# One-hot products on VectorE, and 28 blocks of early scores in plain float32 between the steps of a router

## The chip, the cores and the metric

The kernel runs on one core of a Trainium2 chip. The metric is the time of one execution in microseconds (us), taken on the device; a profile of one execution shows what each engine did. The engines are TensorE (PE; its weight loads are listed apart as PEld), VectorE (DVE), ScalarE (ACT), GpSimd (POOL) and SyncE (SP), which issues most transfers.

## The reference, cut to what matters

The program is a trunk of two layers over 512 tokens with 256 context tokens and 1024 channels. Each layer ends in a mixer with 16384 experts of one neuron each. A token has 8 heads; each head scores two halves of a query against two tables of 128 keys, takes the best 16 of each, combines the sums, and keeps the best 16 pairs as its experts:

```python
        qy = (xb @ w_q).reshape(t, PEER_HEADS, 2, PEER_DKEY // 2)
        s = jnp.einsum('thpd,hpnd->thpn', qy, sub_keys).astype(jnp.float32)
        s_top, i_top = lax.top_k(s, kk)
        comb = (s_top[:, :, 0, :, None] + s_top[:, :, 1, None, :]).reshape(t, PEER_HEADS, kk * kk)
        c_top, c_idx = lax.top_k(comb, kk)
        i1 = jnp.take_along_axis(i_top[:, :, 0], c_idx // kk, axis=-1)
        i2 = jnp.take_along_axis(i_top[:, :, 1], c_idx % kk, axis=-1)
        expert = i1 * PEER_KEYS + i2
        gate = jax.nn.softmax(c_top, axis=-1)
        u = u_tab[expert]
        vv = v_tab[expert]
        act = jax.nn.gelu(jnp.einsum('td,thkd->thk', xb, u).astype(jnp.float32), approximate=False)
        return jnp.einsum('thk,thkd->td', (gate * act).astype(xb.dtype), vv)
```

The kernel must return the latent stream after both layers.

## The kernel before, in words

Work goes by tiles of 128 tokens. For three of the four latent tiles (`ND = 3`, 384 tokens) the mixer isn't done by fetching rows, but densely: `peer_dense` walks over all 128 blocks of 128 experts. For each block it makes the scores of all 384 tokens (`expert_scores`), multiplies the GELU of them by a table of gates that is zero where a token hasn't chosen the expert (`gated`), and adds the products with `v` into six accumulators (`apply`). The fourth tile (and, in layer 0, both context tiles) is done by indirect transfers of single rows on POOL's queue; `pump` releases these gathers at `rate` per dense block, 3 in layer 0 and 2.5 in layer 1, and 2 in a block of `FILL`. Layer 1 ends its gathers with the last blocks; in layer 0 the rest of them runs beside the next mixer.

Float32 products are mostly made of three products in the type fp32r, a rounded form that the operand is split into: `uh` (rounded, on ACT, L1330) and `ul` (the rest, on POOL, L1331); the transposed input `xT` is held as two such parts. A block of scores so has 8 x 3 = 24 matmuls of 384 columns (`sp`), and a block of `apply` 3 x 2 x 3 = 18 of 512 columns (`acc`).

Ahead of the dense blocks stands `peer_route` (names begin with `xp` in layer 0, `yp` in layer 1): four groups of query matmuls and key scores with `top16` on DVE, then for every tile `chosen`, which runs `combine`, then `peer_gates`. `combine` picks indices by a one-hot comparison `oh` (L1180, DVE), a product (L1182, POOL) and a tree of additions (L1185, DVE). `peer_gates` makes the table of gates of a tile in 32 steps `q` of four tokens: a comparison `i2` (L1302, DVE), a comparison `o1` (L1305, DVE), a product `i1` of `o1` and the gates (L1308, POOL; the fourth token by ACT), and four plain float32 matmuls `pg` on PE, copied out by ACT.

The scores of the last 20 blocks (`FILL`) don't depend on the router. They are issued at low priority, in the same split form as in the dense stage, and fill PE's gaps in the router; their GELU goes to DRAM (`gedram`), and the dense stage reads it back, so that these blocks have only `apply` there. Engines take their instructions in program order; a scheduler that sorts by priority sets that order when the program is built.

Of the kernel before, what the change touches and what calls it, by code (L numbers as in the profile page):

```python
# [19 lines left out]
P = 128  # L20
# [7 lines left out]
FILL = range(P - 20, P)  # L28
# [12 lines left out]
class Trunk:  # L41
    def __init__(self, tc, ins, out, dbg=None):
        self.tc = tc
        self.nc = tc.nc
        self.I = ins
        self.out = out
        self.dbg = dbg or {}
        self.flip = 0
        self.queue = []
        self.aside = []  # L50
        self.rate = (3, 2.5)
        self.owed = 0
# [645 lines left out]
    def out_proj(self, yT, w, layer, s, xs, dst, nm, xT, nd):  # L698
# [3 lines left out]
        xh, xl = xT  # L702
        self.h2 = []
        with self.tc.tile_pool(name=nm + "_op", bufs=2, side="right") as tp:
# [35 lines left out]
            def turn(t, h):  # L740
                for g in range(2):
                    p = self.ps(nm + f"_o{t}h2T{g}")
                    for kb in range(4):
                        self.tr(p[:, kb * P:(kb + 1) * P], h[:, (4 * g + kb) * P:(4 * g + kb + 1) * P])
                    d = lambda q: q[:, 4 * g:4 * g + 4, t * P:(t + 1) * P]
                    pv = p.rearrange("p (k t) -> p k t", t=P)
                    nc.scalar.copy(d(xh), pv)
                    nc.vector.tensor_sub(d(xl), pv, d(xh))

# [265 lines left out]
    def peer_route(self, layer, nm, xT, nd, fill=None, beside=iter(())):  # L1015
# [6 lines left out]
        xh, xl = xT  # L1022
        with ExitStack() as st:
# [14 lines left out]
            with ExitStack() as qst:  # L1038
                w3 = qst.enter_context(self.tc.tile_pool(name=nm + "_prw", bufs=2))
                if fill:  # L1040
                    fill()
# [50 lines left out]
                aside(1 << 20)  # L1092
# [23 lines left out]
            with self.tc.tile_pool(name=nm + "_pg", bufs=2) as g2:  # L1116
                for t in order[:nt - nd + 1]:
                    weave(chosen(t))
                for t in range(nd):
                    weave(self.peer_gates(g2, picks, t, nm), *([chosen(t + 1)] if t + 1 < nd else []))  # L1120
        return res
# [10 lines left out]
    def combine(self, pool, p2, V, Iu, ex, gate, hs, nm):  # L1132
# [44 lines left out]
        for q, sel in ((0, isel), (1, jsel)):  # L1177

            oh = pool.tile(sh, BF16, tag=f"oh{q}", name=nm + f"_oh{q}")
            nc.vector.tensor_tensor(oh, sel.rearrange("p (h k) -> p h k", h=n).unsqueeze(2).to_broadcast(sh),  # L1180
                                    self.rank.unsqueeze(1).to_broadcast(sh), op=ALU.is_equal)
            nc.gpsimd.tensor_mul(oh, oh, I4[:, :, q, :].unsqueeze(3).to_broadcast(sh))  # L1182
            yield
            for w in (8, 4, 2):
                nc.vector.tensor_add(oh[:, :, 0:w, :], oh[:, :, 0:w, :], oh[:, :, w:2 * w, :])  # L1185
            nc.vector.tensor_add(ex[:, q, hs], oh[:, :, 0, :], oh[:, :, 1, :])
            yield
# [98 lines left out]
    def peer_gates(self, pool, picks, t, nm):  # L1286
# [8 lines left out]
        for g in range(4):  # L1295
            go = pool.tile([P, P, 32], F32, tag="go", name=nm + f"_go{t}{g}")
            for q in range(8):
# [10 lines left out]
                anchor = nc.gpsimd.tensor_mul(i1[:, 0:3, :], o1[:, :, 0:3].rearrange("p i e -> p e i"),  # L1308
# [8 lines left out]
                if q % 2:  # L1317
                    yield
            nc.sync.dma_start(self.gdram[4 * t + g], go)

    def expert_scores(self, pool, b, xT, layer, nm, ps):
# [3 lines left out]
        ur = pool.tile([P, D], F32, tag="ur", name=nm + f"_ur{b}")  # L1325
        nc.sync.dma_start(ur, self.I[f"peer_uT{layer}"][b])
# [93 lines left out]
    def peer_x(self, xs, dst, xT, layer, nm, done):  # L1420
        with ExitStack() as st:
            up = st.enter_context(self.tc.tile_pool(name=nm + "_du", bufs=2))

            def fill():

                with self.tc.high_priority(offset=-LATER // 2):
                    for i, b in enumerate(FILL):
                        go, _ = self.expert_scores(up, b, xT, layer, nm, self.acc)
                        self.nc.scalar.dma_start(self.gedram[i], go())

            with self.banks(nm + "r", 4, 2, 2):
                r = self.peer_route(layer, nm, xT, ND, fill=fill)
# [5 lines left out]
    def build(self):  # L1438
        nc, tc, I = self.nc, self.tc, self.I
        with ExitStack() as st:  # L1440
# [13 lines left out]
            with ExitStack() as l0:  # L1454
# [174 lines left out]
```

## Time and profile before

| | us |
|---|---|
| median of 3 runs | 4472.95 |
| lowest and highest of them | 4471.51, 4479.77 |
| the profiled execution | 4472.55 |
| its span in the trace | 4470.6 |
| PE, DVE, POOL, ACT busy in it | 3969.2, 3589.9, 2416.3, 1671.3 |

The profiled execution lies 0.4 us under the median, and 1.95 us of its time lie outside the span. In the tables of windows a line gives a stretch of the span, the busy time of each engine with its number of instructions, the clock granted to TensorE as a share of its full speed, the mean busy share of the 16 DMA engines, and what they moved. In a timeline a row gives start, duration, engine, line and operation, output and inputs, and in brackets the idle time before with what ended it; an instruction's recorded duration reaches past the start of the next one on its engine, so the spacing of starts says what it costs in a row of many.

### The profile page before, as it was taken

To read this page: it belongs to the slowest core of one execution; us is meant where nothing else is said; L and a number is where in the kernel's file an instruction comes from. 1 tells how busy PE (TensorE), PEld (TensorE's weight loads), DVE (VectorE), ACT (ScalarE), POOL (GpSimd) and SP (SyncE) were. 2 spreads that over 40 slices of the span, in tenths; PEclk is the share of its full clock that TensorE was granted. 3 is DMA by queue.
4 is the path that set the end of the run, shared out by engine and by line. 5 is a ranking of instruction groups with operands and counts; after the bars stand their busy time and mean duration, and the time that the engine had idled before them with its cause. 6 is when DMAs were issued, how large, how long until landed. Compare 5 with 4: busy or idle time off the path is not lost. (4 is left out here: it accounts for less than half of the span.)

```text
span 4470.6 us, 60041 instructions
## 1 busy us (share of the span) xinstructions
PE 3969.2 (89%) x20898; PEld 3312.4 (74%) x20898; DVE 3589.9 (80%) x6565; ACT 1671.3 (37%) x2981; POOL 2416.3 (54%) x1736
## 2 busy tenths in 40 slices
PE   7988988886786789999999976999767999999998
PEld 4676554784576678998999754776766899999997
DVE  1355889998899989999999876554999788888875
ACT  2354343452224533333333331652345333333333
POOL 0003567545646788767666765002467666666644
PEclk9999999998888999999999997999889999999999
DMA  8825589768822399999999987212224988888875
GB/s 305 293 89 167 195 299 326 265 218 270 290 92 109 164 363 350 346 341 337 336 345 337 319 288 255 65 59 88 71 114 170 354 318 304 306 313 308 308 259 174
DMA packets 480256, 1107.70 MB, mean 248 GB/s; under 512 B 38224, under 2 KB 251728, under 8 KB 470736
## 3 DMA queue, kind: packets, MB, share of 16 engines
q1 hardware_dynamic: 326592, 558.60, 36.0%
q0 software_dynamic: 147600, 537.40, 33.3%
q10 hardware_dynamic: 5760, 7.87, 0.5%
q8 instruction: 164, 2.69, 0.2%
q14 instruction: 140, 1.15, 0.1%
HBM read 1033.41 MB, written 70.78 MB: 247 GB/s over the span
## 5 line engine op out<-in xcount | busy, mean ns | idle before, releaser
L1331 POOL TENSOR_TENSOR yp_ul<-yp_ur,yp_uh 128x1024 fp32r<-128x1024 f32 x128 | 310.3, 2425 | 537.1 <-ACT yp_uh L1330 536.8
L74 PE MATMUL yp_sp<-yp_xT,yp_uh 128*128 128x384 f32 x2048 | 537.8, 343 | 9.8 <-ACT yp_ge L1340 8.3
L74 PE MATMUL xp_sp<-xp_xT,xp_uh 128*128 128x384 f32 x2048 | 536.3, 342 | 9.3 <-ACT xp_uh L1330 8.7
L1331 POOL TENSOR_TENSOR xp_ul<-xp_ur,xp_uh 128x1024 fp32r<-128x1024 f32 x128 | 316.9, 2477 | 162.5 <-ACT xp_uh L1330 161.6
L1221 POOL DMA_INDIRECT cp_v<-peer_v,cp_idx x256 | 311.8, 1218 | 166.4 <-DVE cp_acc L1250 100.1
L74 PEld LDWEIGHTS yp_sp<-yp_xT,yp_uh 128*128 128x128 f32 x2048 | 382.1, 193 | 20.0 <-ACT yp_ge L1340 9.7
L74 PEld LDWEIGHTS xp_sp<-xp_xT,xp_uh 128*128 128x128 f32 x2048 | 380.7, 192 | 18.9 <-ACT xp_uh L1330 9.3
L1221 POOL DMA_INDIRECT cp_u<-peer_u,cp_idx x256 | 319.2, 1247 | 134.2 <-issue 44.5
L74 PE MATMUL xp_sp<-xp_xT,xp_ul 128*128 128x384 f32 x1024 | 351.2, 343 | 21.3 <-POOL xp_ul L1331 21.3
L1378 DVE TENSOR_TENSOR yp_a<-yp_ge,yp_gb 128x384 f32<-128x384 f32 x108 | 257.8, 2387 | 139.9 <-ACT yp_ge L1340 139.9
L74 PE MATMUL yp_sp<-yp_xT,yp_ul 128*128 128x384 f32 x1024 | 352.2, 344 | 16.1 <-POOL yp_ul L1331 16.1
L1250 DVE SCALAR_TENSOR_TENSOR cp_acc<-cp_v,cp_act,cp_acc 128x1024 f32<-128x1024 f32 x254 | 330.5, 1301 | 7.1 <-DMA cp_v<-peer_v,cp_idx 4.4
L74 PE MATMUL xp_acc<-xp_vh,xp_al 128*128 128x512 f32 x768 | 309.3, 403 | 24.8 <-DVE xp_al L1383 23.7
L74 PE MATMUL xp_acc<-xp_vh,xp_ah 128*128 128x512 f32 x768 | 305.4, 398 | 17.3 <-ACT xp_ah L1382 17.3
L74 PE MATMUL xp_acc<-xp_vl,xp_ah 128*128 128x512 f32 x768 | 305.8, 398 | 3.5 <-POOL xp_vl L1370 3.5
L74 PE MATMUL yp_acc<-yp_vh,yp_al 128*128 128x512 f32 x768 | 301.1, 392 | 0.3 <-issue 0.3
L74 PE MATMUL yp_acc<-yp_vl,yp_ah 128*128 128x512 f32 x768 | 300.7, 392 | 0.0
L74 PE MATMUL yp_acc<-yp_vh,yp_ah 128*128 128x512 f32 x768 | 298.8, 389 | 0.3 <-ACT yp_ah L1382 0.3
L1378 DVE TENSOR_TENSOR xp_a<-xp_ge,xp_gb 128x384 f32<-128x384 f32 x108 | 236.2, 2187 | 49.0 <-ACT xp_ge L1340 49.0
L1330 ACT CAST yp_uh<-yp_ur 128x1024 fp32r<-128x1024 f32 x128 | 134.6, 1051 | 327.4 <-issue 235.0
L1330 ACT CAST xp_uh<-xp_ur 128x1024 fp32r<-128x1024 f32 x128 | 134.4, 1051 | 264.4 <-issue 167.4
L74 PEld LDWEIGHTS xp_sp<-xp_xT,xp_ul 128*128 128x128 f32 x1024 | 196.9, 192 | 23.4 <-POOL xp_ul L1331 23.4
(1460 smaller groups left out, 10491.4 us busy)
## 6 DMA issues: line engine op xcount, KB each, us to landing
xp_ur<-peer_uT SPq DMA_DIRECT2D x128, 512.0 KB
xp_vr<-peer_v SPq DMA_DIRECT2D x128, 512.0 KB
yp_ur<-peer_uT SPq DMA_DIRECT2D x128, 512.0 KB
yp_vr<-peer_v SPq DMA_DIRECT2D x128, 512.0 KB
aw<-ada_w SPq DMA_DIRECT2D x48, 1024.0 KB
gdram<-xp_go SPq DMA_DIRECT2D x12, 2048.0 KB
xp_gb<-gdram SPq DMA_DIRECT2D x32, 768.0 KB
gdram<-yp_go SPq DMA_DIRECT2D x12, 2048.0 KB
```

The costliest lines, as they stand in the source:

```text
L74: self.nc.tensor.matmul(out, lhsT, rhs, start=start, stop=stop)
L1221: d = nc.gpsimd.indirect_dma_start(out=r, out_offset=None, in_=tab, in_offset=bass.IndirectOffsetOnAxis(ap=idx[:, j:j + 1], axis=0))
L1250: i = nc.vector.scalar_tensor_tensor(acc, v, act[:, j:j + 1], acc, op0=ALU.mult, op1=ALU.add)
L1330: nc.scalar.copy(uh, uv)
L1331: anchor = nc.gpsimd.tensor_sub(ul, uv, uh)
L1378: nc.vector.tensor_mul(a.rearrange("p (g t) -> p g t", t=32), ge.rearrange("p (g t) -> p g t", t=32), gbs[b // 4][:, :, b % 4, :])
```

## The change

The change has four parts. `FILL` grows from 20 to 28 blocks. The scores of those blocks become 8 plain float32 matmuls per block, of `u` as loaded and of a third, float32 copy of the transposed input (`xT[2]`), without the split on ACT and POOL. They are no longer issued at low priority, but by a generator that `fills(k)` advances by hand: one step at the router's start, two after each step of a tile's choice and two after each pair of steps `q` in the gates, and the rest at the end. A step is one matmul; the block's last one comes with its GELU and its store. The loads of `u` run one block ahead. And the two products on one-hot tables, `oh` in `combine` (16 in each of the two latent routers, 8 in the context one) and `i1` in `peer_gates` (96 in each latent router), move from POOL to DVE.

```diff
-FILL = range(P - 20, P)
+FILL = range(P - 28, P)
...
                     nc.scalar.copy(d(xh), pv)
                     nc.vector.tensor_sub(d(xl), pv, d(xh))
+                    if t < nd:
+                        self.evac(d(xT[2]), pv)
...
-                if fill:
-                    fill()
+                self.fills(1)
...
-                aside(1 << 20)
+                while first:
+                    aside(1)
+                    self.fills(2)
...
                 for t in order[:nt - nd + 1]:
-                    weave(chosen(t))
+                    for _ in chosen(t):
+                        self.fills(2)
                 for t in range(nd):
                     weave(self.peer_gates(g2, picks, t, nm), *([chosen(t + 1)] if t + 1 < nd else []))
+                self.fills(1 << 20)
...
-            nc.gpsimd.tensor_mul(oh, oh, I4[:, :, q, :].unsqueeze(3).to_broadcast(sh))
+            nc.vector.tensor_mul(oh, oh, I4[:, :, q, :].unsqueeze(3).to_broadcast(sh))
...
-                anchor = nc.gpsimd.tensor_mul(i1[:, 0:3, :], o1[:, :, 0:3].rearrange("p i e -> p e i"),
+                anchor = nc.vector.tensor_mul(i1[:, 0:3, :], o1[:, :, 0:3].rearrange("p i e -> p e i"),
                                               pk[:, 2, t0:t0 + 3].unsqueeze(2).to_broadcast([P, 3, P]))
...
                 if q % 2:
+                    self.fills(2)
                     yield
...
+    def load_u(self, pool, b, layer, nm):
+        ur = pool.tile([P, D], F32, tag="ur", name=nm + f"_ur{b}")
+        self.nc.sync.dma_start(ur, self.I[f"peer_uT{layer}"][b])
+        return ur
+
+    def fills(self, k):
+
+        while k and next(self.fill, 0) != 0:
+            k -= 1
...
-                with self.tc.high_priority(offset=-LATER // 2):
-                    for i, b in enumerate(FILL):
-                        go, _ = self.expert_scores(up, b, xT, layer, nm, self.acc)
-                        self.nc.scalar.dma_start(self.gedram[i], go())
-
+                load = lambda b: self.load_u(up, b, layer, nm)
+                nxt = load(FILL[0])
+                yield
+                for i, b in enumerate(FILL):
+                    ur, nxt = nxt, load(b + 1) if i + 1 < len(FILL) else None
+                    sp = self.acc(nm + f"_sp{b}")
+                    for k in range(KD):
+                        self.mm(sp[:, :ND * P], ur[:, k * P:(k + 1) * P], xT[2][:, k, :], start=(k == 0), stop=(k == KD - 1))
+                        if k < KD - 1:
+                            yield
+                    ge = up.tile([P, ND * P], F32, tag="ge", name=nm + f"_ge{b}")
+                    self.nc.scalar.activation(ge, sp[:, :ND * P], AF.Gelu)
+                    self.nc.scalar.dma_start(self.gedram[i], ge)
+                    yield
+
+            self.fill = fill()
```

Where the matmuls stand decides what PE can do while it waits. The first place is PE's program in layer 1 where the first tile's choice is turned round (`pk`) and the gates begin. Here 24 split products a block stand before it, 264 of them since the last key scores:

```order
L74 MATMUL yp_sp_25210<-yp_xT_24532,yp_uh_25206 128x384
L74 MATMUL yp_sp_25210<-yp_xT_24531,yp_ul_25207 128x384
L74 MATMUL yp_sp_25210<-yp_xT_24531,yp_uh_25206 128x384
L77 MATMUL yp_pk_26926<-ident,yp_ex_24813 128x128
L74 MATMUL yp_sp_25210<-yp_xT_24532,yp_uh_25206 128x384
L74 MATMUL yp_sp_25210<-yp_xT_24531,yp_ul_25207 128x384
L74 MATMUL yp_sp_25210<-yp_xT_24531,yp_uh_25206 128x384
L74 MATMUL yp_sp_25210<-yp_xT_24532,yp_uh_25206 128x384
L77 MATMUL yp_pk_26926<-ident,yp_ex_24813 128x128
L77 MATMUL yp_pk_26926<-ident,yp_gate_24817 128x128
L74 MATMUL yp_sp_25210<-yp_xT_24531,yp_ul_25207 128x384
L74 MATMUL yp_sp_25210<-yp_xT_24531,yp_uh_25206 128x384
```

After the change the same place holds plain products with `yp_ur` and `yp_xTf`, and 91 of them stand since the last key scores:

```order
L75 MATMUL yp_sp_26096<-yp_xTf,yp_ur_25932 128x384 x8
L75 MATMUL yp_sp_26233<-yp_xTf,yp_ur_26094 128x384 x8
L78 MATMUL yp_pk_25851<-ident,yp_ex_24297 128x128
L75 MATMUL yp_sp_26353<-yp_xTf,yp_ur_26231 128x384
L78 MATMUL yp_pk_25851<-ident,yp_ex_24297 128x128
L78 MATMUL yp_pk_25851<-ident,yp_gate_24301 128x128
L75 MATMUL yp_sp_26353<-yp_xTf,yp_ur_26231 128x384 x5
L75 MATMUL yp_0_pg<-yp_0_i_25868,yp_0_i_25864 128x128 x4
L75 MATMUL yp_sp_26353<-yp_xTf,yp_ur_26231 128x384
L75 MATMUL yp_4_pg<-yp_4_i_25881,yp_4_i_25877 128x128 x4
L75 MATMUL yp_sp_26353<-yp_xTf,yp_ur_26231 128x384
```

From there on, a fill product stands between most gate products. The second place is PE in the third tile's gates of layer 1, before the change:

```order
L74 MATMUL yp_88_pg<-yp_88_i_28223,yp_88_i_28219 128x128 x4
L74 MATMUL yp_92_pg<-yp_92_i_28236,yp_92_i_28232 128x128 x4
L74 MATMUL yp_96_pg<-yp_96_i_28251,yp_96_i_28247 128x128 x4
L74 MATMUL yp_100_pg<-yp_100_i_28264,yp_100_i_28260 128x128 x4
L74 MATMUL yp_sp_25380<-yp_xT_24532,yp_uh_25376 128x384
L74 MATMUL yp_104_pg<-yp_104_i_28277,yp_104_i_28273 128x128 x4
L74 MATMUL yp_108_pg<-yp_108_i_28290,yp_108_i_28286 128x128 x4
L74 MATMUL yp_112_pg<-yp_112_i_28303,yp_112_i_28299 128x128 x4
L74 MATMUL yp_116_pg<-yp_116_i_28316,yp_116_i_28312 128x128 x4
L74 MATMUL yp_120_pg<-yp_120_i_28329,yp_120_i_28325 128x128 x4
```

and with it:

```order
L75 MATMUL yp_88_pg<-yp_88_i_27302,yp_88_i_27298 128x128 x4
L75 MATMUL yp_sp_27496<-yp_xTf,yp_ur_27480 128x384
L75 MATMUL yp_92_pg<-yp_92_i_27315,yp_92_i_27311 128x128 x4
L75 MATMUL yp_96_pg<-yp_96_i_27332,yp_96_i_27328 128x128 x4
L75 MATMUL yp_sp_27496<-yp_xTf,yp_ur_27480 128x384
L75 MATMUL yp_100_pg<-yp_100_i_27345,yp_100_i_27341 128x128 x4
L75 MATMUL yp_sp_27496<-yp_xTf,yp_ur_27480 128x384
L75 MATMUL yp_104_pg<-yp_104_i_27363,yp_104_i_27359 128x128 x4
L75 MATMUL yp_sp_27496<-yp_xTf,yp_ur_27480 128x384
L75 MATMUL yp_108_pg<-yp_108_i_27376,yp_108_i_27372 128x128 x4
L75 MATMUL yp_112_pg<-yp_112_i_27394,yp_112_i_27390 128x128 x4
```

Before, the gate products stand nearly bare there; now a plain fill product lies between most of them, some 109 over all 96 steps, and 22 to 24 are left before the first `acc`, where 100 split ones were left before. The third place is DVE at the same steps, before:

```order
L1302 TENSOR_TENSOR yp_92_i_28232<-yp_picks_27739,iota 128x512
L1305 TENSOR_TENSOR yp_92_o_28234<-yp_iotam,yp_pb_27926 128x512
L1302 TENSOR_TENSOR yp_96_i_28247<-yp_picks_27739,iota 128x512
L1305 TENSOR_TENSOR yp_96_o_28249<-yp_iotam,yp_pb_27926 128x512
L1302 TENSOR_TENSOR yp_100_i_28260<-yp_picks_27739,iota 128x512
L1305 TENSOR_TENSOR yp_100_o_28262<-yp_iotam,yp_pb_27926 128x512
```

and after, where L1308, L1311 and L1314 are the lines of `i2`, `o1` and the product `i1`:

```order
L1311 TENSOR_TENSOR yp_96_o_27330<-yp_iotam,yp_pb_26965 128x512
L1308 TENSOR_TENSOR yp_100_i_27341<-yp_picks_26755,iota 128x512
L1314 TENSOR_TENSOR yp_96_i_27332<-yp_96_o_27330,yp_picks_26755 128x384
L1311 TENSOR_TENSOR yp_100_o_27343<-yp_iotam,yp_pb_26965 128x512
L1308 TENSOR_TENSOR yp_104_i_27359<-yp_picks_26755,iota 128x512
L1314 TENSOR_TENSOR yp_100_i_27345<-yp_100_o_27343,yp_picks_26755 128x384
L1311 TENSOR_TENSOR yp_104_o_27361<-yp_iotam,yp_pb_26965 128x512
L1308 TENSOR_TENSOR yp_108_i_27372<-yp_picks_26755,iota 128x512
L1314 TENSOR_TENSOR yp_104_i_27363<-yp_104_o_27361,yp_picks_26755 128x384
```

The product has become a third DVE instruction of each step, one step behind its comparison.

## Rows read from the trace of the kernel before

**Rows 1.** Windows of layer 1: choice, gates, transition, normal dense blocks, FILL blocks.

```profile
3185.00:3275.00 90.00, 59.64 (x278) 57.15 (x277) 89.28 (x380) 29.59 (x37) 43.86 (x22) 0.79 0.26 89
3275.00:3457.00 182.00, 137.36 (x887) 118.18 (x886) 178.81 (x290) 99.75 (x207) 129.42 (x105) 0.93 0.36 148
3457.00:3485.00 28.00, 24.73 (x127) 24.09 (x125) 6.78 (x6) 10.69 (x15) 18.80 (x11) 0.88 0.95 357
3485.00:4366.00 881.00, 880.66 (x4451) 801.50 (x4452) 735.60 (x704) 307.66 (x424) 544.47 (x357) 1.00 0.85 305
4366.00:4456.00 90.00, 90.00 (x399) 74.27 (x397) 49.63 (x54) 33.63 (x46) 46.86 (x19) 1.00 0.60 197
```

**Rows 2.** Windows of layer 0: choice and gates, normal dense blocks, FILL blocks.

```profile
1299.00:1571.00 272.00, 195.15 (x1162) 174.55 (x1161) 270.20 (x676) 131.41 (x242) 174.33 (x126) 0.89 0.32 126
1610.00:2525.00 915.00, 895.23 (x4455) 806.12 (x4456) 844.87 (x837) 312.80 (x433) 667.59 (x444) 0.99 0.94 343
2525.00:2648.00 123.00, 99.23 (x395) 75.47 (x393) 111.57 (x87) 30.25 (x41) 101.62 (x59) 0.96 0.90 307
```

**Rows 3.** Timeline of DVE in the choice of layer 1, the two comparisons of one tile.

```profile
3210.11 0.68 DVE L1180 TENSOR_TENSOR yp_c_oh<-yp_c10isel,rank 128x1024 bf16<-128x1024 bf16 x1
3211.07 2.25 DVE L1180 TENSOR_TENSOR yp_c_oh<-yp_c10jsel,rank 128x1024 bf16<-128x1024 bf16 x1
```

**Rows 4.** Timeline of DVE in the gates of layer 0.

```profile
1506.04 0.68 DVE L1302 TENSOR_TENSOR xp_i<-xp_picks,iota 128x512 f32<-128x512 f32 x1
1506.65 1.04 DVE L1305 TENSOR_TENSOR xp_o<-xp_iotam,xp_pb 128x512 bf16<-128x512 bf16 x1
1507.62 0.68 DVE L1302 TENSOR_TENSOR xp_i<-xp_picks,iota 128x512 f32<-128x512 f32 x1
```

**Rows 5.** Lines L1305 and L1308 in layer 1 (min/median/max in ns).

```profile
L1305 DVE TENSOR_TENSOR yp_o<-yp_iotam,yp_pb x96: 401/1045/2582, 3273.3 to 3453.0; 128x512 bf16<-128x512 bf16 x96
...
L1308 POOL TENSOR_TENSOR yp_i<-yp_o,yp_picks x96: 826/1146/1391, 3273.8 to 3454.1; 128x384 f32<-128x384 bf16 x96
```

**Rows 6.** Timeline of PE in the same gates of layer 0.

```profile
1504.32 1.16 PE L74 MATMUL xp_pg<-xp_i,xp_i 128*128 128x128 f32 x8 [0.41 <-POOL xp_i L1308]
```

**Rows 7.** Timeline of PE in a normal dense block, first and last products.

```profile
4303.86 0.51 PE L74 MATMUL yp_sp<-yp_xT,yp_uh 128*128 128x384 f32 x2
...
4308.05 0.39 PE L74 MATMUL yp_acc<-yp_vh,yp_ah 128*128 128x512 f32 x1
...
4311.94 0.39 PE L74 MATMUL yp_acc<-yp_vh,yp_al 128*128 128x512 f32 x1
```

**Rows 8.** Groups of DVE in the choice, layer 1 (count, busy us, mean ns).

```profile
L1185 DVE TENSOR_TENSOR yp_c_oh<-yp_c_oh 128x512 bf16<-128x512 bf16 x9 | 12.1, 1346 | 0.0
L1185 DVE TENSOR_TENSOR yp_c_oh<-yp_c_oh 128x256 bf16<-128x256 bf16 x10 | 9.0, 904 | 0.0
```

**Rows 9.** Timeline of DVE: the same forms at their shortest, later.

```profile
3375.11 0.41 DVE L1185 TENSOR_TENSOR yp_c_oh<-yp_c_oh 128x512 bf16<-128x512 bf16 x1
3376.68 0.28 DVE L1185 TENSOR_TENSOR yp_c_oh<-yp_c_oh 128x256 bf16<-128x256 bf16 x1
```

**Rows 10.** Timeline of DVE, products of 384 and 1024 elements elsewhere.

```profile
2734.67 0.55 DVE L823 TENSOR_TENSOR m_qr_t<-m_qr_rot,sin 128x384 f32<-128x384 f32 x1
2735.14 0.55 DVE L824 TENSOR_TENSOR m_qrt<-m_qrt,cos 128x384 f32<-128x384 f32 x1
...
2764.10 1.22 DVE L1253 TENSOR_TENSOR xp_acc<-xp_acc,xp_g 128x1024 f32<-128x1024 f32 x1
```

**Rows 11.** Timeline and window of PE: 12 plain float32 products; timeline: first turn in layer 1.

```profile
2738.71 7.90 PE L74 MATMUL m_qn<-cqT,m_wuq 128*128 128x384 f32 x24
...
2738.50:2747.00 8.50, 8.12 (x26) 4.45 (x24) 8.43 (x13) 0.83 (x2) 4.87 (x4) 1.00 0.97 319
...
3269.71 0.45 PE L77 MATMUL yp_pk<-ident,yp_ex 128*128 128x128 f32 x1 [8.84 <-DVE yp_ex L1186]
```

**Rows 12.** Gathers of layer 0 left behind the dense stage (line L1221, count, first, last).

```profile
L1221 POOL DMA_INDIRECT xp_v<-peer_v,xp_idx x44: 944/1244/1962, 2669.4 to 2754.0; - x44
```

More of the change, by code (lines that the diff above doesn't have):

```diff
@@ L49, in __init__ @@
         self.queue = []
+        self.fill = iter(())
         self.aside = []
@@ L701, in out_proj @@
         nc = self.nc
-        xh, xl = xT
+        xh, xl = xT[:2]
         self.h2 = []
@@ L1012, in odd_mixer, with peer_route @@
         return xT
-    def peer_route(self, layer, nm, xT, nd, fill=None, beside=iter(())):
+    def peer_route(self, layer, nm, xT, nd, beside=iter(())):
         nc = self.nc
@@ L1021, in peer_route @@
         res = []
-        xh, xl = xT
+        xh, xl = xT[:2]
         with ExitStack() as st:
@@ L1324, in expert_scores @@
         n = ND * P
-        ur = pool.tile([P, D], F32, tag="ur", name=nm + f"_ur{b}")
-        nc.sync.dma_start(ur, self.I[f"peer_uT{layer}"][b])
+        ur = self.load_u(pool, b, layer, nm)
         uh = pool.tile([P, KD, P], F32R, tag="uh", name=nm + f"_uh{b}")
@@ L1424, in fill @@
             def fill():
-                with self.tc.high_priority(offset=-LATER // 2):
-                    for i, b in enumerate(FILL):
-                        go, _ = self.expert_scores(up, b, xT, layer, nm, self.acc)
-                        self.nc.scalar.dma_start(self.gedram[i], go())
+                load = lambda b: self.load_u(up, b, layer, nm)
[13 more added lines that the diff above has]
+            self.fill = fill()
             with self.banks(nm + "r", 4, 2, 2):
-                r = self.peer_route(layer, nm, xT, ND, fill=fill)
+                r = self.peer_route(layer, nm, xT, ND)
             with self.banks(nm + "d", 2, 6):
@@ L1474, in f @@
                         p = st.enter_context(tc.tile_pool(name=name, bufs=1))
-                        return [p.tile([P, KD, n], F32R, name=name + str(j)) for j in range(2)]
+                        return [p.tile([P, KD, n], F32R, name=name + str(j)) for j in range(2)] + \
+                            ([p.tile([P, KD, ND * P], F32, name=name + "f")] if n == NX else [])
                     return f
```

## The prediction

> **What bounds the kernel now.** I cut the span of layer 1 into windows at the places where a stage's first instruction stands, then read timelines inside them. In the normal dense blocks PE is busy for 880.66 of 881 us and in the `FILL` blocks for 90.00 of 90, at full clock [rows 1]: these are bound by PE, and what leaves PE leaves the time. Between the last key scores and the first `acc` it is otherwise. In the choice (90 us) DVE is busy for 89.28 and PE for 59.64; in the gates (182 us) DVE for 178.81 and PE for 137.36; in the transition (28 us) PE has most, 24.73 [rows 1]. So the router's 300 us hang on DVE for 272 and on PE for 28. Layer 0 has the same for choice and gates, 272 us with DVE at 270.20 [rows 2]. Its dense stage differs: with three gathers a block DVE and the DMA engines are nearly full too (915 us for 108 blocks, 8.5 a block), and in `FILL` DVE has 111.57 and POOL 101.62 of 123 us, PE only 99.23: the gathers pace it.
>
> DVE's busy time in the router is not all work. The comparison `oh` of one tile takes 0.68 us, and its twin, while POOL runs the product on the first, 2.25 [rows 3]. In the gates `o1` takes 0.40 us at its shortest and 1.05 in the median, with POOL's `i1` at 1.15 [rows 5]. In the steady part a step costs 0.61 for `i2` and 0.97 for `o1`, 1.58 together [rows 4], and PE waits 0.41 us of it for POOL's `i1` [rows 6]. DVE and POOL hold each other up there.
>
> **Price of a score block.** The 24 split products take 4308.05 - 4303.86 = 4.19 us, and the 18 of `acc` (4311.94 - 4308.05) / 17 x 18 = 4.12 [rows 7], so a normal block is 8.3 and a `FILL` block 4.1. The trace has plain float32 products of 384 columns: 24 records, two for each product, in 7.90 us at granted clock 1.00 [rows 11]. Less the last one's tail (some 0.17) that is 0.322 a record, 0.644 a product, 5.15 us a block of 8. By itself a plain block is 0.96 dearer than a split one, where PE is the bound.
>
> The row has two records for a product that costs 3.7 times one of the split products (0.175). [...] I take the row's 5.15.
>
> **Router, choice (L1 90 us).** Off DVE go the mutual waits: three `oh` comparisons at 2.3 instead of 0.68 make 4.9 us [rows 3]; the additions L1185 of 512 and 256 elements average 1.346 and 0.904 us here against 0.41 and 0.28 at their shortest, so 9 x 0.94 + 10 x 0.62 = 14.7 [rows 8, 9]. Other forms have some of it too; I count none. On DVE come 8 products `oh`. Two bounds: 0.60 us, the comparison of the same size, and 1.22, a 1024-element product in float32 [rows 3, 10]. An operand that is repeated over 16 elements makes the second nearer: 8 x 1.2 = 9.6. DVE then has 89.3 - 19.6 + 9.6 = 79; with the mutual waits that I didn't count I take 73 as the middle between that and 67. PE has 91 plain products, 58.6 us, and an idle end like the 8.84 us ahead of the first turn [rows 11]: 67. So 73, a gain of 17; bounds 67 and 79.
>
> **Gates (L1 182 us).** The nearest row for `i1` on DVE is a float32 product of 384 elements: 0.55 recorded, 0.47 from start to start [rows 10]; from above, POOL's own shortest, 0.83 [rows 5]. The size, the output type and the engine agree with the first, so 0.47. A step on DVE is then 0.61 + 0.33 (`o1`, 0.40 recorded) + 0.47 = 1.40, and 96 of them 134. What else stands on DVE there is 178.8 - 96 x 1.58 = 27, and 4 products `oh` add 5, less some waiting: in all 162 to 166. PE has 96 steps of four gate products, recorded as 1.16 with a tail of some 0.2 [rows 6], so about 1.0 each and 96 in all, and 109 fill products at 0.644, 70: 166. The two engines are level, at 165, a gain of 17. POOL, with neither `ul` nor `i1`, has nearly nothing left there. ACT loses 20 casts `uh` and keeps the copies; it was busy for 99.75 of 182.
>
> **Transition (28 us).** Of 148 split products ahead of the first `acc` some 100 belonged to `FILL`: 17.5 us; now 22 plain ones, 14.2, plus nothing else new: 3 less. The loads of 28 blocks, 512 KB each, fall into stages with a DMA share of 0.26 and 0.36 [rows 1], which cover them.
>
> Layer 1's router: -17 - 17 - 3 = -37. Layer 0's has the same counts within three products and the same windows: -36, for a transition that waits more on its loads.
>
> **Dense, layer 1.** Eight blocks lose 24 split products: 8 x 4.19 = -33.5. Gathers: 8 blocks now get 2 instead of 2.5, and about 6 of 256 land in `FILL` blocks. Layer 0's `FILL` blocks show what two gathers do to a block without scores: 123 us for 22 groups of `acc`, 5.6 instead of 4.1 [rows 2, 1], 0.75 a gather: +4.5. Together -29.
>
> **Dense and tail, layer 0.** Eight blocks go from 8.5 to 5.6: -23. But each releases one gather less, so 8 more of the 512 slots stay behind the dense stage. There 44 of them stand at (2754.0 - 2669.4) / 43 = 1.97 us [rows 12], and the next mixer waits for the last: +16. Together -7. The gain of this stage is mostly handed to the tail.
>
> **Small parts.** The six extra evacuations of `xT[2]` a layer stand at the end of a projection: +1 in all. The context router's 8 products move beside the latent mixer, which keeps PE busy: 0.
>
> **Sum**: -37 - 36 - 29 - 7 + 1 = -108. The profiled execution is 4472.55, 0.4 under the median, so 4472.55 - 108 = 4365.
>
> **Rivals.**
> (B) More of DVE's time was waiting, and PE isn't in the way: choice 63, gates 155 (DVE's 134 and 21), so -27 - 27 - 4 = -58 a router and 4365 - 43 = 4322. For it: L1185 is not the only form that is long beside POOL. Against: PE's own count of 166 in the gates.
> (C) `i1` on DVE costs what it cost on POOL, since it reads `o1` across its rows: 0.83. A step is 0.61 + 0.33 + 0.83 = 1.77, the gates 170 + 30 = 200, 18 longer than now; a router is then -17 + 18 - 3 = -2 and the time 4472.55 - 4 - 35 = 4434. The gates lose from (182 - 30) / 96 - 0.94 = 0.64 us on. For it: no row has this stride on DVE.
> (D) PE is dearer than the row: its granted clock, 0.79 in the choice and 0.93 in the gates [rows 1], stays as low. Then 58.6 / 0.79 + 8.8 = 83 and 166 / 0.93 = 178, 10 + 13 more a router: 4365 + 46 = 4411. Against: the clock is low there where PE waits, and the fill products now stand between the waits. [...]
> (E) Slower. PE takes its instructions in order, and now a fill product stands between most gate products. A block whose `ur` hasn't landed holds up the gate products behind it, and with them the copies on ACT and the four buffers of `i1` that DVE writes. Each of 56 blocks has a load of 512 KB with only one block's lead. It decides from 108 / 56 = 1.9 us of open wait a block; at 4 us it gives 4365 + 224 = 4589. Against: a block's 8 products are spread over some 8 steps of 1.4 to 1.7 us, so a load has over 11 us, and the DMA engines are two thirds idle.
>
> **Chances.** Forecast 0.62, B 0.10, C 0.11, D 0.12, E 0.05. The range 4325 to 4412 takes in D and the bounds of the choice (6 each way and router) and leaves out C, E and half of B, 0.2. A measurement of this kernel tells about 0.2%, 9 us. All but E, and the edge of C with a dearer `oh` too, lie below that: faster 0.94, same 0.02, slower 0.04.
>
> **What the profile after would show.** Right: windows of choice and gates of about 73 and 165 us a layer, with PE over 0.9 busy in the gates; `o1` near 0.4 and `i1` on DVE near 0.55 recorded; plain fill products 0.64 apart; layer 1's dense part 29 shorter; the end of layer 0's gathers no more than 10 earlier after the router's gain is taken off. Wrong: `i1` at 0.8 or more (C), PE idle ahead of `yp_sp` with a DMA of `yp_ur` as releaser (E), fill products 0.7 or more apart at full clock, or a granted clock of 0.8 in the gates (D).

## The result, and the profile after

The changed kernel takes 4371.97 us (median of 4 runs, 4360.89 to 4380.56) against 4476.01 before: ratio 0.9771, 95% interval 0.9757 to 0.9784. Forecast were 4365 and a range of 4325 to 4412. The profiled execution took 4360.89, 11 under the median and 111.7 less than the profiled one of before, while the medians differ by 104; differences of a few us between stages of two profiles mean little, above all in layer 0's dense stage.

Windows of layer 1 after the change, with the columns of [rows 1]: choice, gates, transition, normal dense blocks, `FILL` blocks.

```profile
3133.10:3206.20 73.10, 65.50 (x200) 37.99 (x199) 72.35 (x388) 19.96 (x29) 2.23 (x1) 0.95 0.37 119
3206.20:3361.60 155.40, 155.06 (x974) 124.02 (x973) 154.16 (x390) 96.94 (x208) 0.00 (x0) 1.00 0.56 210
3361.60:3392.00 30.40, 25.28 (x95) 18.13 (x95) 7.31 (x4) 9.07 (x13) 10.24 (x7) 0.94 0.89 311
3392.00:4210.20 818.20, 815.40 (x4118) 740.66 (x4117) 692.16 (x672) 284.57 (x392) 523.74 (x346) 1.00 0.87 312
4210.20:4344.80 134.60, 126.60 (x541) 101.85 (x541) 87.23 (x80) 44.97 (x62) 75.03 (x33) 0.99 0.66 222
```

The same five of layer 0, for [rows 2]:

```profile
1286.40:1358.90 72.50, 65.78 (x202) 38.53 (x201) 72.32 (x383) 19.56 (x29) 2.23 (x1) 0.95 0.36 111
1358.90:1515.20 156.30, 155.75 (x978) 124.89 (x977) 156.27 (x396) 97.81 (x209) 1.54 (x1) 1.00 0.55 209
1515.20:1563.80 48.60, 29.15 (x100) 20.80 (x99) 28.11 (x40) 9.25 (x12) 25.62 (x20) 0.75 1.00 367
1563.80:2403.30 839.50, 820.96 (x4117) 740.82 (x4117) 780.23 (x775) 283.89 (x393) 626.50 (x410) 1.00 0.94 344
2403.30:2570.20 166.90, 137.67 (x542) 107.42 (x540) 157.01 (x118) 43.08 (x57) 138.76 (x83) 0.93 0.93 320
```

In the choice DVE is the engine without a gap, as before, but it needs 73 us instead of 90 [rows 1]; PE is busy for 65.50 of them. In the gates PE (155.06) and DVE (154.16) are both full for 155.40 us and POOL does nothing at all. Groups by line in layer 1, for [rows 5], show the price of a comparison, of `i1` and of `oh` on DVE (min/median/max in ns):

```profile
L1311 DVE TENSOR_TENSOR yp_o<-yp_iotam,yp_pb x96: 394/418/423, 3203.9 to 3359.4; 128x512 bf16<-128x512 bf16 x96
L1314 DVE TENSOR_TENSOR yp_i<-yp_o,yp_picks x96: 528/551/558, 3204.8 to 3359.8; 128x384 f32<-128x384 bf16 x96
L1188 DVE TENSOR_TENSOR yp_c_oh<-yp_c_oh,yp_c_If x13: 1209/1212/1220, 3146.4 to 3287.3; 128x1024 bf16<-128x1024 bf16 x13
```

The comparison's longest is now 423 ns where its median was 1045. Timelines of DVE and of PE in the gates, for [rows 4, 6]: a step is 1.40 us from `o1` to `o1`, a pair of plain records 0.64.

```profile
3300.19 0.42 DVE L1311 TENSOR_TENSOR yp_o<-yp_iotam,yp_pb 128x512 bf16<-128x512 bf16 x1
3300.52 0.69 DVE L1308 TENSOR_TENSOR yp_i<-yp_picks,iota 128x512 f32<-128x512 f32 x1
3301.12 0.55 DVE L1314 TENSOR_TENSOR yp_i<-yp_o,yp_picks 128x384 f32<-128x384 bf16 x1
3301.59 0.42 DVE L1311 TENSOR_TENSOR yp_o<-yp_iotam,yp_pb 128x512 bf16<-128x512 bf16 x1
```

```profile
3305.87 0.81 PE L75 MATMUL yp_sp<-yp_xTf,yp_ur 128*128 128x384 f32 x2
3306.51 2.06 PE L75 MATMUL yp_pg<-yp_i,yp_i 128*128 128x128 f32 x16
3308.42 0.81 PE L75 MATMUL yp_sp<-yp_xTf,yp_ur 128*128 128x384 f32 x2
```

### The profile page after: what moved, and what is told of

Its sections match the earlier page's. It is cut to its first block, busy times and chain, and to the rows that moved or that the text cites. A ratio compares the mean times of both kernels' runs of the same rounds, so it can differ in the third digit from the quotient of the medians.

```text
span 4359.1 us, 58568 instructions
## 1 busy us (share of the span) xinstructions
PE 3943.7 (90%) x20450; PEld 3198.6 (73%) x20450; DVE 3497.9 (80%) x6787; ACT 1613.3 (37%) x2929; POOL 2035.1 (47%) x1467
## 4 chain that ended last, share of the span: by engine, by line
PE 61%; DVE 20%; DMA 8%; issue 6%; ACT 2%; POOL 2%; SPq 0%; DVEq 0%; ACTq 0%; POOLq 0%
PE yp_acc L75 10%; PE yp_sp L75 10%; PE xp_sp L75 9%; PE xp_acc L75 8%; PE mq_s L75 2%; DVE cp_acc L1256 2%; DMA cp_u<-peer_u,cp_idx 2%; PE x_p L75 1%; DVE cp_jk L1245 1%; PE yp_pg L75 1%; PE xp_pg L75 1%; DVE xp_acc L1256 1%; PE ada_ps L75 1%; PE yp_qy L75 1%; PE c_p L75 1%
## 5 line engine op out<-in xcount | busy, mean ns | idle before, releaser
L1347 POOL TENSOR_TENSOR yp_ul<-yp_ur,yp_uh 128x1024 fp32r<-128x1024 f32 x100 | 242.0, 2420 | 421.1 <-ACT yp_uh L1346 421.0
L75 PE MATMUL xp_sp<-xp_xT,xp_uh 128*128 128x384 f32 x1600 | 409.7, 337 | 12.4 <-ACT xp_uh L1346 12.4
L75 PE MATMUL yp_sp<-yp_xT,yp_uh 128*128 128x384 f32 x1600 | 408.8, 336 | 1.4 <-ACT yp_ge L1453 1.4
L1347 POOL TENSOR_TENSOR xp_ul<-xp_ur,xp_uh 128x1024 fp32r<-128x1024 f32 x100 | 249.6, 2496 | 130.0 <-ACT xp_uh L1346 129.5
L75 PEld LDWEIGHTS xp_sp<-xp_xT,xp_uh 128*128 128x128 f32 x1600 | 293.2, 189 | 20.6 <-ACT xp_uh L1346 13.0
L75 PEld LDWEIGHTS yp_sp<-yp_xT,yp_uh 128*128 128x128 f32 x1600 | 292.4, 188 | 9.7 <-ACT yp_ge L1453 2.0
L75 PE MATMUL yp_sp<-yp_xT,yp_ul 128*128 128x384 f32 x800 | 269.4, 337 | 3.2 <-POOL yp_ul L1347 3.2
L75 PE MATMUL xp_sp<-xp_xT,xp_ul 128*128 128x384 f32 x800 | 269.8, 337 | 1.4 <-POOL xp_ul L1347 1.4
L1057 POOL TENSOR_TENSOR yp_wql<-yp_wq,yp_wqh 128x1024 fp32r<-128x1024 f32 x16 | 38.7, 2420 | 369.1 <-DMA yp_wq<-peer_w_q 311.5
L1398 ACT CAST xp_ah<-xp_a 128x384 fp32r<-128x384 f32 x128 | 65.8, 514 | 367.7 <-DVE xp_a L1394 323.5
```

The costliest lines, as they stand in the source:

```text
L75: self.nc.tensor.matmul(out, lhsT, rhs, start=start, stop=stop)
L1057: self.pump(nc.gpsimd.tensor_sub(wl, raw, wh), 0)
L1347: anchor = nc.gpsimd.tensor_sub(ul, uv, uh)
L1398: nc.scalar.copy(ah, a)
```

## The experiments

My theory after the result: DVE and POOL hold each other up in the router, whatever the POOL operation is for, and taking all POOL work out of it (the split's subtractions and the products) is what freed DVE. Rivals: the gain lies in who places the fill products; or in the eight blocks; or the parts simply add.

The times of stages below are those between the PE instructions that bound a stage, from start to start, in one profiled execution of each kernel (the choice from the last key scores to the first gate product, the transition from the last gate product to the first `acc`); cut so, the stages of before are up to 2.5 us longer or shorter than the rounder windows of [rows 1]. The last column is the ratio of a kernel's time to that of before on the same chip.

| us | L1 choice | L1 gates | L1 transition | L1 dense | L0 transition | L0 dense | L0 dense end to L1 queries | ratio |
|---|---|---|---|---|---|---|---|---|
| before | 92.5 | 180.3 | 29.1 | 970.9 | 39.6 | 1037.9 | 419.7 | 1 |
| changed | 73.1 | 155.4 | 30.4 | 952.8 | 48.6 | 1006.4 | 446.6 | 0.9771 |
| DVE products alone | 91.5 | 172.7 | 21.7 | 966.1 | 28.0 | 1039.4 | 420.3 | 0.9901 |
| plain fills alone | 76.1 | 172.2 | 56.0 | 948.8 | 56.2 | 986.4 | 448.1 | 0.9993 |
| dummy on POOL | 83.4 | 172.5 | 31.0 | 956.6 | 47.0 | 1011.9 | 450.1 | 0.9950 |
| `oh` on POOL | 77.2 | 156.6 | 53.1 | 949.6 | 80.7 | 993.6 | 447.3 | 0.9880 |
| placed by scheduler | 73.3 | 154.7 | 34.7 | 951.3 | 47.8 | 1009.6 | 445.2 | 0.9771 |
| 20 blocks | 73.2 | 160.4 | 23.2 | 966.6 | 27.8 | 1035.3 | 438.1 | 0.9795 |
| 36 blocks | 73.2 | 154.5 | 72.9 | 930.3 | 108.4 | 966.8 | 465.6 | 0.9878 |
| context early | 73.1 | 155.2 | 32.0 | 952.1 | 46.8 | 1019.7 | 438.9 | 0.9775 |
| rates, context early | 73.1 | 155.4 | 30.9 | 941.4 | 46.4 | 1020.1 | 428.7 | 0.9722 |
| paced | 73.1 | 155.0 | 29.1 | 941.7 | 46.5 | 1014.5 | 430.5 | 0.9698 |
| 25 blocks, paced | 73.1 | 156.8 | 28.1 | 950.8 | 33.1 | 1016.8 | 432.3 | 0.9719 |
| 25 and 28, paced | 73.2 | 154.9 | 30.3 | 942.9 | 33.1 | 1024.2 | 432.3 | 0.9706 |

**The two parts apart.** Into the kernel before, the two products alone:

```diff
-            nc.gpsimd.tensor_mul(oh, oh, I4[:, :, q, :].unsqueeze(3).to_broadcast(sh))
+            nc.vector.tensor_mul(oh, oh, I4[:, :, q, :].unsqueeze(3).to_broadcast(sh))
...
-                anchor = nc.gpsimd.tensor_mul(i1[:, 0:3, :], o1[:, :, 0:3].rearrange("p i e -> p e i"),
+                anchor = nc.vector.tensor_mul(i1[:, 0:3, :], o1[:, :, 0:3].rearrange("p i e -> p e i"),
```

> The kernel before with only the two one-hot products moved from POOL to DVE; the scores of 20 FILL blocks stay split and at low priority. Theory A (DVE and POOL hold each other up in choice and gates, and taking the products off POOL ends most of it; the split's subtractions on POOL are left and still hold DVE up some 2 us each): a step of the gates falls from 1.58 us to about 1.4 to 1.5, the choice from 92 us to about 80, the gates from 180 to about 160, so some 30 a router, in all 60 less than before, 4416 (4395 to 4435). Rival B (the router's gain came from the fill products placed between the gate products): 10 less at most, 4465. Under either the dense stages and the end of layer 0's gathers stay as before.

And the changed kernel with those two lines turned back:

> The changed kernel with both one-hot products back on POOL. Theory A: the gates keep POOL's product in each step, 1.5 to 1.58 us a step and 175 to 180 us, and the choice loses only the waits for the subtractions, about 85 instead of 92; dense stages as in the changed kernel, 18 and 5 net less than before. In all about 30 less than before, 4445 (4430 to 4455). Rival B (placing the fill products brings the router's gain): routers as in the changed kernel, 4375 to 4390.

Measured: 4434.94, ratio 0.9901 (0.9884 to 0.9919), 41 less, at the slow edge of what theory A gave; and 4470.85, ratio 0.9993 (0.9983 to 1.0003), no change, where A gave 30 less and B some 90. Together they bring 104. Windows of choice and gates in layer 1 with the products alone:

```profile
3167.80:3259.30 91.50, 73.94 (x370) 71.09 (x370) 91.32 (x379) 35.14 (x45) 38.03 (x16) 0.89 0.34 112
3259.30:3432.00 172.70, 132.27 (x880) 118.11 (x880) 169.99 (x396) 97.17 (x205) 38.79 (x11) 0.94 0.44 174
```

The choice is as long as before and not the 80 us of theory A: the subtractions are still there (POOL 38 us), and DVE needs 91.32 us for its 379 instructions, where the changed kernel, with POOL at 2.23, needs 72.35 for 388. The gates are 8 us shorter and not 20; much of the gain, 7 and 12 us, lies in the two transitions. With the fills alone it is the reverse: the choice is short without the subtractions although `oh` is on POOL, the gates keep POOL's product, and fewer plain products stand ahead of the last gate, so that 60 come behind it (windows of choice, gates, transition):

```profile
3199.60:3275.70 76.10, 55.90 (x157) 31.74 (x157) 75.64 (x385) 18.00 (x25) 18.47 (x12) 0.87 0.27 86
3275.70:3447.90 172.20, 153.78 (x941) 123.25 (x940) 168.22 (x287) 97.01 (x208) 113.88 (x99) 0.97 0.48 181
3447.90:3503.90 56.00, 50.31 (x171) 31.61 (x170) 5.90 (x5) 11.60 (x17) 9.63 (x6) 0.97 0.93 312
```

In layer 0 its gates take 224.8 us, 68 more than in the changed kernel, and that is most of what this run lacks; 20 come back in layer 0's dense stage. Groups of DVE and POOL there show context gathers that the changed kernel, but for one, doesn't run until the gates are over. Why they come earlier here was not tried:

```profile
L1245 DVE SCALAR_TENSOR_TENSOR cp_jk<-cp_u,c_o1h 128x1024 bf16<-128x1024 f32 x29 | 38.8, 1340 | 0.0
L1227 POOL DMA_INDIRECT cp_u<-peer_u,cp_idx x27 | 31.1, 1151 | 56.9 <-DVE cp_jk L1245 40.5 <-PE xp_pg L75 6.9 <-ACT xp_go L1322 5.4
```

**One useless POOL operation per block.**

```diff
+                    dz = up.tile([P, D], F32, tag="dz", name=nm + f"_dz{b}", bufs=1)
+                    self.nc.gpsimd.tensor_sub(dz, ur, ur)
```

> The changed kernel with one useless subtraction of 128x1024 float32 on POOL for each of the 28 FILL blocks in a layer (the size of the split's subtraction, its result read by nothing), and two instead of three residual buffers at the end of the dense stages to make room for it. Theory A (a POOL operation holds DVE up for its own time, whether anybody waits for its result or not): some 12 of them fall into the choice and 13 into the gates of each layer, at 2.4 us each, of which about 1.5 to 2 is lost to DVE; choice 73 to about 93, gates 155 to about 175, so 40 a router and 80 in all, 4450 (4420 to 4470). Rival B (what helped is only that PE, ACT or DVE no longer wait for a POOL result): within 10 us of the changed kernel.

Measured: 4459.14, ratio 0.9950 (0.9933 to 0.9967), some 80 slower than the changed kernel. In layer 1 the choice is 10 longer and the gates 17, with 12 of the operations in each; layer 0 has 11 and 17. Windows of choice and gates in layer 1:

```profile
3184.90:3268.30 83.40, 68.43 (x201) 39.29 (x199) 82.64 (x386) 19.86 (x28) 26.21 (x13) 0.90 0.33 104
3268.30:3440.80 172.50, 158.71 (x974) 125.43 (x973) 171.50 (x389) 97.08 (x208) 75.90 (x12) 0.99 0.50 186
```

The line of the operation in the gates (min/median/max in ns), and DVE's timeline where two of them stand:

```profile
L1449 POOL TENSOR_TENSOR yp_dz<-yp_ur x12: 1907/2108/31510, 3275.4 to 3439.5; 128x1024 f32<-128x1024 f32 x12
```

```profile
3324.05 2.25 DVE L1314 TENSOR_TENSOR yp_i<-yp_o,yp_picks 128x384 f32<-128x384 bf16 x1
3326.23 2.38 DVE L1308 TENSOR_TENSOR yp_i<-yp_picks,iota 128x512 f32<-128x512 f32 x1
```

Nobody reads the result, yet DVE's 0.55 and 0.68 become 2.25 and 2.38, and one POOL operation stretches to 31.5 us in gates where DVE is busy for 171.50 of 172.50. Most instructions of a step are as long as in the changed kernel: the medians of `o1`, `i2` and `i1` are 0.41, 0.68 and 0.55 us, there 0.42, 0.68 and 0.55. The longest are 2.12, 2.38 and 2.25, and in the gates the three lines have some 16 us more than as many instructions at the medians of the changed kernel, nearly all of the 17 by which the stage is longer. The row of a POOL operation of 12.65 us, and the row of DVE just ahead of the two above:

```profile
3313.24 12.65 POOL L1449 TENSOR_TENSOR yp_dz<-yp_ur 128x1024 f32<-128x1024 f32 x1 [14.37 <-DMA yp_ur<-peer_uT]
3323.92 0.22 DVE L1300 CAST yp_pb<-yp_picks 128x128 bf16<-128x128 f32 x1
```

From 3313.24 on some 23 DVE instructions follow one another at their usual lengths. The two behind the cast are 1.70 us longer than usual each; this POOL operation ends at 3325.89, in the first of them, and the next one at 3328.05, in the second. Three of the 12 POOL operations are that long (12.7, some 13.9 and 31.5 us from start to end), the other nine take some 1.9 to 2.3. What decides when one of them ends was not tried. PE waits 13.5 us in these gates for DVE's `i1` and not at all for `ur`, so later loads aren't the cause. Rival B of this run falls. The two routers together are 55 us longer, where theory A gave 80. The rest of the 80 is outside them (4.5 of it behind the dense end of layer 1, where the residual buffers went from three to two) and wasn't taken apart.

**`oh` alone back on POOL.** (Its line as in the diff above, turned back; 16 operations a layer.)

> The changed kernel with the product of combine (16 a layer) back on POOL and that of the gates left on DVE. Theory A (a product on POOL holds DVE up about as long as DVE itself takes for it, 1.2 us, and some more): choice 76 as in the run with both products on POOL, gates 2 to 4 longer; 8 to 18 slower than the changed kernel, 4384. Rival B (the product is free on POOL or dear on DVE): level or faster, 4355 to 4372.

Measured: 4423.46, ratio 0.9880 (0.9864 to 0.9897), 49 slower, far beyond either. Choice and gates of layer 1 are only 4 and 1 longer. The windows show where the rest is:

```profile
3173.10:3250.30 77.20, 57.88 (x160) 32.75 (x159) 76.73 (x389) 18.52 (x26) 16.98 (x10) 0.86 0.27 85
3250.30:3406.90 156.60, 150.37 (x958) 121.59 (x957) 151.51 (x379) 96.38 (x207) 12.92 (x4) 1.00 0.54 203
3406.90:3460.00 53.10, 46.35 (x152) 30.25 (x151) 6.35 (x5) 11.01 (x17) 10.04 (x6) 0.90 0.93 320
```

PE's program has 77 plain products in the choice instead of 97, and 50 instead of 22 behind the last gate: 23 us there in layer 1, 32 in layer 0. The scheduler that sets the order placed them later. Why it did was not tried.

**Who places the products.**

```diff
-                self.fills(1)
+                with self.tc.high_priority(offset=-LATER // 2):
+                    self.fills(1 << 20)
```

> The changed kernel with all steps of the fill generator taken at the router's start at the old low priority, so that the scheduler places the plain products and not the two-per-step calls. Theory A (what counts is that the products are plain and off POOL, not who places them): within 15 us of the changed kernel, 4372 (4360 to 4390). Rival B (the placing by hand gives the gates' gain): gates 10 to 20 longer in each layer, 4395 to 4415.

Measured: 4380.5 with 4481.69 before on that chip, ratio 0.9771 (0.9755 to 0.9787), that of the changed kernel. The two-per-step calls bring nothing by themselves; B falls. That holds with POOL all but idle in the router (2.23 us busy in layer 1's choice, 0.00 in its gates); with `oh` on POOL the run above shows what late places cost.

**Number of blocks.** `FILL = range(P - 20, P)` and `range(P - 36, P)`.

> The changed kernel with FILL of 20 blocks instead of 28. Theory A (the changed router is near both bounds, so 64 plain products less a layer save only what stands after the last gate, some 10 to 15 us, and choice and gates stay at 73 and 154 to 156; each dense stage gets its 8 full blocks back, 18 longer in layer 1, and in layer 0 31 longer with a tail that is 13 shorter): 5 to 15 slower than the changed kernel, about 4384. Rival C (PE bounds the whole changed router, so 64 products of 0.644 give 41 back in each): faster than the changed kernel by about 45, 4327. Rival D (the 8 blocks rode for nothing): slower by 36, 4408.

> The changed kernel with FILL of 36 blocks. Theory A (at 28 PE is full in the gates at 155 us and DVE too, so eight more blocks find no room): 64 more products of 0.645, 41 us, come behind the last gate in each layer; the dense stages give back 18 in layer 1 and 31 less 13 to 20 in the tail of layer 0: about 45 slower than the changed kernel, 4415 (4400 to 4430). Rival B (there is still room in the router): 10 to 30 faster, 4345 to 4360.

Measured: 4382.77, ratio 0.9795 (0.9778 to 0.9811), 11 slower; and 4427.48, 0.9878 (0.9861 to 0.9894), 48 slower: the times are A's both times. With 20 the gates don't stay at 154 to 156, as A had it, but are 5 longer although PE has 40 products less there; DVE is full for all of it, and POOL work has moved up beside it (gates of layer 1, 11.66 instead of 0.00: two subtractions for the first dense blocks, 6.2 us, and five gathers). That these are what lengthens the gates is argued, not shown. The window:

```profile
3213.00:3373.40 160.40, 142.27 (x890) 116.16 (x889) 160.40 (x392) 96.42 (x205) 11.66 (x7) 0.96 0.54 204
```

With 36, choice and gates are unchanged and everything added stands behind them, as the window of layer 1's transition shows:

```profile
3410.70:3483.60 72.90, 66.21 (x223) 40.33 (x222) 6.63 (x5) 13.10 (x21) 9.99 (x6) 1.00 0.81 270
```

**Behind layer 0's dense stage.** Before, the first gather there came 22 us after its end, now 35; the last 106, now 133. The third copy of `xT` moved the stage's last buffers onto the context rows of the next mixer, whose loads came at 1067.9 and 2051.4 before. The loads in the changed kernel, and the row of PE that waits for them:

```profile
L112 SPq DMA_DIRECT2D mc_x<-c x2: 320/376/432, 2578.6 to 2579.0; - x2
```

```profile
2588.62 3.86 PE L78 MATMUL mc_hT<-ident,mc_x 128*128 128x128 f32 x16 [18.03 <-ACT mc_x L230]
```

```diff
-                    x = tp.tile([P, D], F32, tag="x", name=nm + f"_dx{t}", bufs=3)
+                    x = tp.tile([P, D], F32, tag="x", name=nm + f"_dx{t}", bufs=2 + layer)
```

> The changed kernel with two instead of three buffers for the residual rows at the end of layer 0's dense stage. The third copy of the transposed input takes 12 KB a partition and pushed the last buffers of that stage up into the place of the context rows of the next mixer, whose loads came 14 us later behind the dense end than before, at 2578.6 instead of 1067.9 and 2051.4. With two buffers the places no longer overlap. Theory A (the late context rows delay the first gather behind the dense stage by 13.7 us, and the last by as much): loads of the context rows back ahead of the dense end, first gather 22 us behind it instead of 36, and 10 to 14 us less than the changed kernel, about 4360. Rival B (the gathers' own pace or other loads of the mixer's start set it): within 4 us of the changed kernel.

Measured: 4373.44, ratio 0.9775 (0.9759 to 0.9792), no change: B's number. The loads move as A has it and the gain isn't there. They go back into the dense stage:

```profile
L112 SPq DMA_DIRECT2D mc_x<-c x2: 326/462/597, 1578.1 to 2010.4; - x2
```

The first gather comes 25 us behind the dense end and the last 124, 8.5 sooner, and the stage up to layer 1's queries is 8 shorter; but the normal blocks of layer 0 take 852 instead of 840. In both runs with the early context rows they do; in the others with 28 blocks and both products on DVE they take 840 to 844. That the norm's own work is what lengthens them is argued, not shown.

**Release of the gathers.** First together with the line above, then without it:

```diff
-        self.rate = (3, 2.5)
+        self.rate = (3, 2.625)
...
-                self.pump(anchor, self.rate[layer] if b not in FILL else 2)
+                self.pump(anchor, self.rate[layer] if b not in FILL else 3 - layer)
```

> The changed kernel with three gathers instead of two for each FILL block of layer 0, 2.625 instead of 2.5 for each normal block of layer 1, and two residual buffers in layer 0. Theory A (28 fewer slots are left behind the dense stage of layer 0, at 1.9 us each 53 less, for 28 blocks that DVE makes 1.3 longer, 36 more; layer 1's gathers end ahead of its FILL blocks, 8 less): about 25 less than the changed kernel, 4347 (4335 to 4360). Rival B (a FILL block with three gathers is as long as a normal one, 8.5, or layer 1's normal blocks grow past PE's bound): no gain or up to 25 slower.

> The changed kernel with three gathers instead of two for each FILL block of layer 0 and 2.625 instead of 2.5 for each normal block of layer 1, the residual buffers left at three. Theory A (the earlier release of gathers made the gain of the run with both; the two residual buffers moved the context norm into the dense stage of layer 0, where it cost the 12 us that it saved behind it): layer 1's FILL blocks 11 shorter, normal blocks of layer 0 at 840 and not 852, the last gather no more than 130 behind the dense end; 12 to 25 less than the changed kernel, 4355 (4345 to 4362). Rival B (the early context norm made the gain of layer 0): layer 1's 11 alone, 4361 to 4368.

Measured: 4356.31, ratio 0.9722 (0.9706 to 0.9738), 22 less than the changed kernel; and 4340.64, ratio 0.9698 (0.9682 to 0.9714), the best of all, 33 less and so beyond the 12 to 25 of its theory A. The early context rows weren't what gained. In the second run layer 1's `FILL` blocks take 123.8 us instead of 134.6, layer 0's stage behind the dense end 430.5 instead of 446.6, its last gather 104 behind the end instead of 133. The reason given for layer 0, 28 fewer gathers left behind its dense stage, isn't what came: 46 are left there instead of 52, and they start 1 us behind the end instead of 35. By the stages of the two profiled executions the gain is 19; the rest of the 33 is the 11 us by which the changed kernel's profiled execution lies under its median, and scatter.

> The same pacing with FILL of 25 blocks. Choice and gates hold 200 plain products by the count of the changed kernel, which are 25 blocks, so nothing is left behind the last gate. Theory A (in layer 0 the transition falls from 48 to about 28 us as with 20 blocks, in layer 1 from 30 to 23, and three normal blocks come back in each dense stage, 8 longer in layer 1 and 11 in layer 0, with 3 slots less in the tail, 6): about 15 less than with 28 blocks, 4342 (4335 to 4352). Rival B (subtractions on POOL for the first dense blocks move into the gates, as with 20 blocks, and make them 5 longer): level with 28 blocks within 8 us.

> The paced kernel with FILL of 25 blocks in layer 0 and 28 in layer 1. Theory A (each layer keeps the number that was better for it in its own stages: layer 0's transition was 13 shorter with 25, its gates 2, its dense stage and tail 4 longer; layer 1 lost 9 in its dense stage with 25): 5 to 9 less than the paced kernel, 4334 (4328 to 4340). Rival B (stages trade these against each other from run to run, and the two are level): 4338 to 4345.

Measured: 4350.65, ratio 0.9719 (0.9702 to 0.9735), and 4345.71, ratio 0.9706 (0.9690 to 0.9722). Layer 0's transition falls by 13 both times, where 20 and 13 were expected. With 25 in both layers, layer 1's dense stage is 9 longer; with 25 in layer 0 alone, layer 0's dense stage is 10 longer than in the paced run, against 2 in the run before it. Neither beats 28 in both; the interval of the last overlaps that of the paced run.

## Why the prediction was right, and where its terms were off

The mechanism held: DVE's waits went out of both routers, the choice was left to DVE and the gates to DVE and PE at one level, the clock stayed at 1.00 in the gates (D falls), `i1` cost 0.55 recorded and 0.47 from start to start (C falls), and no fill product in the gates waited for its `ur` (E falls; the one such wait of note, 5.6 us, is in layer 0's transition). B's price for the gates, 155, was the right one, though PE was level there too; its 63 for the choice was not.

| term | forecast | measured, layer 1 and 0 |
|---|---|---|
| choice | -17 | -19, -20 |
| gates | -17 | -25, -23 |
| transition | -3, -2 | +1, +9 |
| dense, layer 1 | -29 | -18 |
| dense, layer 0 | -23 | -31 |
| its tail | +16 | +27 |

That the total came within 7 us of 4365 is in part luck: choice, gates and layer 0's dense stage gained 28 us more than forecast, transitions, layer 1's dense stage and the tail 37 less. The measured terms sum to -99; the other 12 of the profiled difference lie ahead of layer 0's choice. The last key scores there start at 1286.4 us in the changed kernel, at 1298.8 before, and at 1289.2 to 1302.8 in the other runs, so these 12 are within the scatter between kernels.

- **Choice.** 73 was the middle between two bounds, not a sum. The waits that left DVE were 30 us in layer 1, by the 19 gained and the 10.9 of 9 products `oh` in their place; the prediction had counted 19.6.
- **Gates.** 27 was put down for what else DVE has there, 5 for `oh`, and 162 to 166 for the sum; 155.4 less 96 steps of 1.40 leaves 21 for both. PE's gate products cost 0.95 a step (16 records, two steps, from 3306.51 to 3308.42) and not 1.0, and about 101 plain products fall into the gates and not 109, 97 into the choice and not 91.
- **Price of a plain block.** 5.15 held: the two records of a product take 0.64 us (3305.87 to 3306.51), 3.7 times a split product's 0.175 [rows 7]. What that factor is made of isn't shown.
- **`oh`.** 1.2 held: 1.21 us for the product, as the float32 row's 1.22 [rows 10], and not the 0.68 of the comparison of the same size and type [rows 3]. That the operand read 16 times is the reason was an estimate; no run has the product without the repetition.
- **Transition, layer 0.** It was counted as layer 1's, but PE waits there 5.6 us for a load of `ur` and 12.4 for the first `uh`, at a DMA share of 1.00 and a granted clock of 0.75. With 25 blocks the stage is 33 us and with 20 it is 28, so the products behind the last gate and their loads are what lengthens it.
- **Layer 1's dense stage.** Six gathers in `FILL` were costed at 4.5; taken out by the paced run, they were worth 11. The other 4 of the 11 that are missing weren't taken apart.
- **Dense stage, layer 0.** The 8 us more than forecast lie in the normal blocks, 8.40 each instead of 8.47; why stays open.
- **Tail.** The sum left out the late context rows. With 20 blocks, the old number of slots, and the same third copy the tail is 438.1, so the copy and what came with it cost 18, and eight slots 8.5 against 16 forecast (19 for the next eight, with 36 blocks). Taking the late rows away gave 8 back there and nothing in the end.

The one step of the reasoning that the runs correct: I priced the products and the fills as terms that add. Alone they brought 41 us and nothing clear of noise, together 104. Either one leaves POOL work that holds DVE up: with the products alone the choice and the gates stay long (91.5 and 172.7 us, POOL busy for 38.03 and 38.79), with the fills alone the gates (172.2 us, POOL 113.88). The rest of the shortfall of the fills alone is in what the order of the program put elsewhere, the 60 products behind the last gate and the context gathers in layer 0's gates; why the order changes with the engine of the products isn't shown.

## What to carry to other kernels

Where DVE and POOL hold each other up, moving a part of POOL's work away may bring far less than its share (here 41 us and nothing, of 104): look for the stage in which POOL would be idle altogether, and cost the parts together. Filler on PE pays only up to the time that the other engine needs anyway (here 155 us in the gates, and eight more blocks made the kernel 48 slower); count what stands behind the last product that had to wait. One more buffer can move a neighbour's place in memory (here loads went from 1067.9 and 2051.4 us to 2578.6), and work released by a count per block shifts when blocks are moved: look at the first instructions behind the stage.

## What the runs showed of the hardware that I had not expected

A POOL operation that nobody waits for took 31.5 us instead of 1.9 in gates where DVE was busy for 171.50 of 172.50 us, and beside such operations DVE's `i1` and `i2` took up to 2.25 and 2.38 instead of 0.55 and 0.68: the wait goes both ways and isn't shared evenly. The rest of DVE's rows in the gates were as long as without POOL (the median of `o1` 0.41, without 0.42). By the length of the stage DVE lost 1.4 us to each of the 12 operations in the gates and 0.9 to each of the 12 in the choice. At 28 blocks DVE and PE were both over 0.99 busy for 155 us (154.16 and 155.06 of 155.40) with POOL at nothing.
